# Moving one load in a hand-written order: step 6's rows right behind step 4's

## The chip, the cores and the metric

The kernel runs on one core of one Trainium2 chip. The metric is the device time of one execution in microseconds (us), lower is better. The core has five engines with queues of their own: TensorE (PE in the profile; its weight loads are PEld), VectorE (DVE), ScalarE (ACT), GpSimd (POOL) and SyncE (SP). Each runs its instructions strictly in the order in which the program was written; they meet only through semaphores. Transfers between the chip's main memory and its on-chip memory are issued by SyncE, GpSimd and once by ScalarE, and are carried by 16 DMA engines.

## The reference

A 3x3 convolution with zero padding, 64 channels in and 128 out, on 16 images of 64x64, then a 2x2 maximum pool:

```python
for b, co, ci, kh, kw:                       # conv is [16, 128, 64, 64]
    conv[b, co] += weight[co, ci, kh, kw] * x_pad[b, ci, kh:kh+h, kw:kw+w]
...
output[b, c, i, j] = np.max(conv[b, c, 2*i:2*i+2, 2*j:2*j+2])   # [16, 128, 32, 32]
```

## The kernel before

Two images share the 128 partitions (2 x 64 channels). The work is cut into 32 steps; a step is a pair of images and a quarter of the rows (16 rows of input, 8 rows of pooled output), and its two images are its halves 0 and 1. The even and the odd rows of a step's convolution differ only in which taps meet which rows, so the kernel multiplies sums and differences of input rows with sums and differences of taps instead of computing both rows in full. There are two kinds of steps, by the string `TYPES`:

- K steps (0, 2, 5, 7, 10, ...) read rows that were cast to bf16 on the way in (`kx`, loaded by `LK` through GpSimd's queue), and need one row sum, `KS` (line 356, VectorE).
- W steps (1, 3, 4, 6, 8, 9, 11, 12, ...) read f32 rows (`wx`, loaded through SyncE's queue at line 137) and make three bf16 operands of them: `E`, the difference of even and odd rows (line 407; on VectorE for steps 3, 8, 9 and 15, on GpSimd for the others), `D`, the difference of rows two apart (line 416, GpSimd), and `WS`, the sum of even and odd rows (VectorE, lines 374, 387 or 395). For steps 4, 6, 8, 14, 17, 22 and 23 ScalarE first copies the odd rows into a bank of PSUM (`XC`, line 370), and `WS` adds that copy (line 374).

Two successive W steps share one of six `wx` buffers: 1 and 3, 4 and 6, 8 and 9, 11 and 12, 14 and 15, 16 and 17; then the buffers are used again (19 and 20 in the first, 22 and 23 in that of 4 and 6). The load of the first of a pair has 18 rows (17 at the top of an image), that of the second 16 (15 at the bottom).

TensorE (line 252) runs the products `PA1`, `PA2`, `PB1`, `PB2`, `PR` of K steps and `P2`, `P0`, `P3`, `P1` of W steps; each is three matmuls of one half, and a product of half 0 is issued interleaved with the next product of half 1, so a pair of products is six matmuls. There are eight banks of PSUM. `EV` (lines 468 and 470, ScalarE) copies a bank out and frees it, `SE` (481, ScalarE) seeds another, `MX` (498, VectorE) takes the maximum of even and odd rows, `OD` (502, ScalarE) copies odd columns out, `CM` (508, VectorE) takes the maximum over columns and frees the bank, and `ST` (516, 519, SyncE) stores the result. A product that starts a bank waits for whoever freed it: P2.4.0 for EV.5.1, for instance, and P2.6.1 for CM.5.1. The numbers are the step and the half.

The order of all this is one text, `ORDER`, written out by hand: a token a step of work, and each engine gets its instructions in the order of the tokens. Loads are `L` and `LB`, both `wload` (line 129). `LB` adds one wait: the load is issued behind the VectorE operation that was last put on record (`on_vector`, line 87: `KS`, the halves `Ea` and `Eb` of step 1's `E`, the `E` of VectorE, and `WS` of line 395 among them) where the token stands. A `D` or `E` of GpSimd waits for the last recorded VectorE operation in the same way (`on_gpsimd`). The W loads before the change come in the order 1, 3, 11, 4, 8, 6, 9, 14, 12, 16, 22, 20 and so on; `LB.4` waits for `KS.0`, `LB.8` and `LB.6` both for `Eb`, and `LB.9` for `E.3`.

```python
def late_load(s):
    behind(wload(s), sbuf_op[0])
```

The products of the first two steps are written in halves (`F`, `G`). Of the steps around the moved load, ScalarE runs OD.3.1, XC.6, XC.4, EV.5.1 in this order; VectorE runs CM.1.1, CM.2.1, CM.3.1, WS.6, WS.4, KS.5, WS.9, KS.7, CM.3.0; GpSimd runs E.4, D.4, E.6, LK.1.0, D.8, D.6, D.9.

Of the kernel before, what the change touches and what calls it, by code (L numbers as in the profile page):

```python
# [11 lines left out]
def kernel(  # L12
# [556 lines left out]

    ORDER = """  # L570
        g2 D2 g0 TD2 D0 TD0 XOa TG0 VD2 F.0.0 GS TG2 g1 XOb VG0 GM F.1.0 uG1 XEb LB.3 VD0 F.0.1 F.1.1 GP VG2 XEa
        EV.0.1 L.11 X2 X1 LK.0.0 uGM F.2.0 PA1.2.0 KS.0 LB.4 Ea uGP F.3.0 TG1 KS.2 F.2.1 TMP Eb F.3.1 PA1.2.1
# [3 lines left out]
        SE.3.0 P0.3.0 EV.3.1 MX.1.1 P3.3.1 P1.1.1 OD.2.0 MX.2.1 E.11 P3.3.0 MX.3.1 ST.0 PR.2.1 P1.3.1 OD.1.0
        EV.3.0 PA1.5.0 PA1.5.1 E.4 OD.1.1 CM.2.0 CM.1.0 MX.3.0 CM.1.1 OD.2.1 PA2.5.1 PB1.5.0 P1.3.0 L.14 PB2.5.0
        D.4 OD.3.1 XC.6 PA2.5.0 E.6 CM.2.1 L.12 P2.4.1 P2.4.0 CM.3.1 XC.4 PA1.7.0 LK.1.0 EV.5.1 PB1.5.1 WS.6
        PB2.5.1 WS.4 L.16 SE.4.1 OD.3.0 PA2.7.0 P0.4.1 KS.5 P3.4.1 WS.9 KS.7 D.8 EV.5.0 SE.4.0 PA1.7.1 CM.3.0
        EV.4.1 EV.7.0 P0.4.0 PA2.7.1 MX.5.1 D.6 P3.4.0 MX.5.0 PR.5.0 MX.4.1 P2.6.0 PR.5.1 EV.4.0 PB1.7.0 MX.4.0  # L580
        XC.8 E.8 P1.4.1 EV.7.1 OD.5.1 P1.4.0 PB1.7.1 OD.4.1 WS.8 PB2.7.1 D.9 OD.5.0 PB2.7.0 SE.6.0 CM.5.1 CM.4.1
        P0.6.0 CM.5.0 OD.4.0 P2.6.1 SE.6.1 MX.7.1 P2.8.1 L.22 MX.7.0 EV.6.0 L.20 CM.4.0 SE.8.1 P3.6.0 PR.7.0
        PR.7.1 P0.6.1 OD.7.1 MX.6.0 EV.6.1 OD.7.0 P2.8.0 E.9 P3.6.1 SE.8.0 P0.8.1 CM.7.1 P1.6.0 P3.8.1 MX.6.1
        E.12 EV.8.1 CM.7.0 P2.9.0 ST.2 OD.6.0 CM.6.0 SE.9.0 P0.8.0 P1.6.1 ST.4 MX.8.1 P3.8.0 P2.9.1 EV.8.0 ST.5
        MX.8.0 L.19 P0.9.0 D.11 P2.11.0 OD.6.1 L.15 CM.6.1 PA1.13.1 P1.8.1 EV.9.0 ST.6 L.25 KS.13 P1.8.0 SE.9.1
        PA2.13.1 SE.11.0 P3.9.0 LK.1.1 KS.10 P0.11.0 D.12 E.14 P0.9.1 OD.8.0 WS.11 EV.13.1 P3.11.0 MX.9.0 P3.9.1
        PA1.10.1 D.14 P1.9.0 OD.8.1 EV.9.1 CM.8.0 CM.8.1 MX.9.1 EV.11.0 P2.12.1 XC.14 PA2.10.1 OD.9.0 MX.11.0
        P1.9.1 L.17 PA1.13.0 E.19 SE.12.1 CM.9.0 P2.11.1 PA2.13.0 P0.12.1 P1.11.0 EV.10.1 EV.13.0 P2.14.0
        PA1.10.0 OD.9.1 WS.14 PA2.10.0 SE.11.1 P3.12.1 P0.11.1 WS.12 EV.12.1 CM.9.1 OD.11.0 MX.12.1 P3.11.1
        P1.12.1 SE.14.0 CM.11.0 ST.1 EV.11.1 P2.12.0 E.15 SE.12.0 P0.14.0 PB1.10.1 P3.14.0 PB2.10.1 MX.11.1  # L590
        EV.14.0 E.16 MX.14.0 D.16 P0.12.0 XC.22 P1.11.1 P3.12.0 P1.14.0 EV.10.0 L.24 EV.12.0 P2.14.1 PB1.10.0
        D.15 WS.22 ST.3 OD.11.1 PB1.13.1 MX.10.1 PB2.10.0 PB2.13.1 MX.12.0 OD.12.1 CM.11.1 P1.12.0 OD.14.0 L.23
        CM.12.1 CM.14.0 SE.14.1 PR.10.1 PA1.21.0 E.17 P0.14.1 MX.13.1 MX.10.0 PA2.21.0 OD.12.0 PR.13.1 PR.10.0
        OD.10.1 CM.10.1 XC.17 EV.14.1 CM.12.0 OD.13.1 WS.17 P3.14.1 EV.21.0 OD.10.0 CM.13.1 P2.15.1 L.27 MX.14.1
        P2.15.0 P2.16.1 PA1.18.0 L.28 SE.15.0 CM.10.0 P1.14.1 PA2.18.0 SE.15.1 P0.15.1 E.20 SE.16.1 ST.12.0 ST.12.1
        P0.15.0 EV.18.0 WS.16 OD.14.1 P3.15.0 WS.15 P3.15.1 P0.16.1 KS.18 EV.15.0 LK.2.0 ST.10 PB1.13.0 P2.16.0
        CM.14.1 EV.15.1 MX.15.0 MX.15.1 EV.16.1 P3.16.1 SE.16.0 PB2.13.0 P2.17.1 MX.16.1 P1.15.1 P1.15.0 SE.17.1
        P0.16.0 OD.15.1 MX.13.0 P1.16.1 PR.13.0 EV.16.0 P3.16.0 D.17 WS.20 P0.17.1 P3.17.1 OD.16.1 P2.17.0
        CM.15.1 CM.16.1 MX.16.0 PA1.18.1 ST.11 OD.13.0 P2.19.0 EV.17.1 PA2.18.1 OD.15.0 CM.13.0 P1.16.0 SE.17.0
        EV.18.1 P0.17.0 P2.20.1 P3.17.0 OD.16.0 D.20 SE.20.1 MX.17.1 PB1.18.0 P1.17.1 D.19 CM.15.0 EV.17.0  # L600
        PA1.21.1 CM.16.0 WS.19 SE.19.0 P0.20.1 E.24 OD.17.1 MX.17.0 E.23 PA2.21.1 EV.20.1 PB2.18.0 MX.18.0
        P3.20.1 ST.7 P0.19.0 P1.17.0 PB1.18.1 EV.21.1 PR.18.0 XC.23 OD.17.0 CM.17.1 P2.19.1 MX.20.1 E.22 P3.19.0
        P2.20.0 EV.19.0 D.23 OD.18.0 WS.23 PB2.18.1 CM.17.0 CM.18.0 P2.23.0 SE.19.1 MX.19.0 MX.18.1 P1.20.1
        OD.20.1 ST.15 P0.19.1 P1.19.0 KS.21 L.31 P3.19.1 SE.20.0 P0.20.0 EV.19.1 D.22 P3.20.0 PR.18.1 OD.19.0
        ST.8.0 ST.8.1 SE.23.0 P0.23.0 CM.20.1 P2.22.1 MX.19.1 EV.20.0 P3.23.0 CM.19.0 OD.18.1 SE.22.1 MX.20.0 P1.19.1
        D.24 CM.18.1 P1.20.0 EV.23.0 PB1.21.1 OD.19.1 P0.22.1 PB2.21.1 OD.20.0 MX.23.0 CM.19.1 P2.22.0 P1.23.0
        CM.20.0 P2.23.1 ST.16.0 ST.16.1 ST.13 EV.22.1 MX.21.1 PB1.21.0 ST.19 SE.22.0 KS.26 ST.17 P0.22.0 L.30 PB2.21.0
        SE.23.1 WS.28 P3.22.1 PR.21.1 OD.23.0 CM.23.0 E.27 P0.23.1 P3.23.1 P2.24.0 EV.22.0 MX.22.1 EV.23.1
        MX.21.0 P3.22.0 OD.21.1 P1.22.1 SE.24.0 OD.22.1 P2.24.1 PR.21.0 MX.23.1 P0.24.0 E.25 OD.21.0 P3.24.0
        P1.23.1 CM.21.1 SE.24.1 CM.22.1 ST.20.0 ST.20.1 EV.24.0 D.25 D.27 MX.22.0 P2.25.1 OD.23.1 D.28 P0.24.1 CM.21.0  # L610
        SE.25.1 P3.24.1 WS.24 CM.23.1 E.28 P1.22.0 OD.22.0 CM.22.0 ST.23 PA1.26.0 PA2.26.0 P0.25.1 WS.25 P2.25.0
        P3.25.1 EV.24.1 EV.26.0 EV.25.1 PB1.26.0 MX.24.1 PA1.26.1 MX.25.1 PA2.26.1 SE.25.0 PB2.26.0 P2.27.1
        MX.26.0 P1.25.1 EV.26.1 P0.25.0 EV.25.0 P3.25.0 SE.27.1 MX.24.0 PR.26.0 P1.24.1 P0.27.1 OD.25.1 P3.27.1
        OD.24.1 OD.26.0 P1.24.0 OD.24.0 MX.25.0 CM.25.1 P2.27.0 CM.24.1 P1.25.0 CM.26.0 ST.22 P2.28.1 EV.27.1
        WS.27 PB1.26.1 E.30 PB2.26.1 CM.24.0 SE.27.0 OD.25.0 P2.28.0 SE.28.1 CM.25.0 SE.28.0 E.31 P0.27.0
        MX.27.1 P0.28.1 P1.27.1 P3.28.1 EV.27.0 MX.26.1 P3.27.0 ST.21 EV.28.1 MX.27.0 P0.28.0 D.30 PR.26.1
        P3.28.0 OD.27.1 P1.27.0 EV.28.0 ST.25 CM.27.1 P2.30.0 MX.28.1 PA1.29.0 P2.30.1 OD.26.1 CM.26.1 OD.27.0
        P1.28.1 SE.30.0 PA1.29.1 KS.29 OD.28.1 CM.27.0 PA2.29.0 P0.30.0 PA2.29.1 SE.30.1 MX.28.0 P0.30.1 EV.29.0
        ST.26 P1.28.0 P2.31.1 P3.30.0 EV.29.1 OD.28.0 CM.28.1 EV.30.0 P2.31.0 WS.31 CM.28.0 P3.30.1 D.31 WS.30
        EV.30.1 PB1.29.1 MX.30.0 PB2.29.1 ST.24 PB1.29.0 MX.30.1 PB2.29.0 MX.29.0 SE.31.0 ST.18 SE.31.1 MX.29.1  # L620
# [50 lines left out]
```

## Time and profile before

| | us |
|---|---|
| median of 3 runs (lowest, highest) | 104.76 (104.11, 105.74) |
| the profiled execution, its own time | 104.74 |
| its span, first to last instruction | 102.9 |
| TensorE busy | 96.5 (94%) |
| VectorE busy | 90.0 (87%) |
| ScalarE busy | 86.0 (84%) |
| GpSimd busy | 79.8 (77%) |
| mean traffic of the DMA engines | 236 GB/s, 24.25 MB |

The profile is one execution on the chip, with a start and a length for every instruction and the semaphores that released it. "A <- B: total, times, longest" says that A waited for B. A line of the timeline has the start, the length, the engine, the line of the code, the operation, output and inputs, the count of instructions merged into it, and in brackets how long the engine had stood idle before and what ended that. A busy TensorE isn't TensorE at its peak, since matmuls overlap in its pipeline. A list of DMA issues gives the median time from issue to landing, the landing being the last of the 16 engines' reports.

### The profile page before, as it was taken

Reading aid. Unit: us, or ns where it says so; the run is one execution under the profiler, and the core shown is the slowest. Engines: PE = TensorE matmul, PEld = TensorE weight load, DVE = VectorE, ACT = ScalarE, POOL = GpSimd, SP = SyncE. Lnnn points to the kernel's source line nnn. Section 1 sums busy time; section 2 is a strip of 40 time slices with the busy share of each in tenths; the row PEclk is TensorE's granted clock in tenths of the full one; section 3 lists DMA queues with packets and bytes.
Section 4 is the critical chain, followed back from the end, with each engine's and each line's share of the span. In section 5 each row is a group of like instructions: output and inputs, shape, how many; then the busy total and the mean of one; then the engine's idle time right before and its main releaser. Section 6 shows DMA issues by size and latency. Waiting matters only on the chain.

```text
span 102.9 us, 2528 instructions
## 1 busy us (share of the span) xinstructions
PE 96.5 (94%) x904; PEld 58.8 (57%) x904; DVE 90.0 (87%) x175; ACT 86.0 (84%) x192; POOL 79.8 (77%) x67
## 2 busy tenths in 40 slices
...
DMA packets 13789, 24.25 MB, mean 236 GB/s; under 512 B 1104, under 2 KB 9296, under 8 KB 13776
## 3 DMA queue, kind: packets, MB, share of 16 engines
...
q0 software_dynamic: 1104, 2.23, 13.4%
q8 instruction: 7, 0.11, 0.5%
...
HBM read 17.92 MB, written 8.39 MB: 256 GB/s over the span
## 4 chain that ended last, share of the span: by engine, by line
PE 78%; DMA 10%; DVE 3%; ACT 3%; issue 1%; DVEq 0%; SPq 0%; ACTq 0%
PE acc L252 73%; DMA wx<-in_x_dram 10%; PE acc L628 3%; PE acc L198 2%; DVE o L508 1%; ACT ev L468 1%; ACT kx L533 1%; DVE acc L498 1%; ACT acc L370 1%; DVE ks L356 0%; DVE we L407 0%; DVE we L428 0%; DVEq L666 0%; SPq L137 0%; DVEq L498 0%
## 5 line engine op out<-in xcount | busy, mean ns | idle before, releaser
L252 PEld LDWEIGHTS <-wt 64*128 64x128 bf16 x870 | 55.8, 94 | 35.2 <-issue 3.3
L252 PE MATMUL acc<-wd,wt 64*128 64x504 bf16 (+3 forms) x276 | 53.9, 367 | 0.0
L416 POOL TENSOR_TENSOR wd<-wx 128x1024 bf16<-128x1024 f32 x21 | 49.3, 2361 | 3.3 <-DVE ks L356 3.1
L252 PE MATMUL acc<-kx,wt 64*128 64x504 bf16 (+6 forms) x264 | 45.0, 351 | 0.0
L498 DVE TENSOR_TENSOR acc<-acc,ev 128x512 f32<-128x512 f32 x64 | 42.0, 689 | 1.6 <-PE acc L252 1.1
L252 PE MATMUL acc<-we,wt 64*128 64x512 bf16 (+3 forms) x138 | 31.8, 367 | 1.3 <-ACT ev L468 1.2
L252 PE MATMUL acc<-ws,wt 64*128 64x512 bf16 (+1 forms) x132 | 32.5, 377 | 0.0
L470 ACT ACTIVATE ev<-acc 128x512 f32<-128x512 f32 x44 | 26.2, 611 | 2.1 <-PE acc L252 1.7
L481 ACT COPY acc<-acc 128x512 f32<-128x512 f32 x42 | 24.5, 593 | 1.9 <-PE acc L252 0.9
L508 DVE TENSOR_TENSOR o<-acc,od 128x256 f32<-128x256 f32 x64 | 24.9, 414 | 1.1 <-ACT od L502 0.9
L502 ACT COPY od<-acc 128x256 f32<-128x256 f32 x64 | 23.2, 384 | 2.5 <-PE acc L252 2.0
L407 POOL TENSOR_TENSOR we<-wx 128x512 bf16<-128x512 f32 x17 | 21.4, 1273 | 4.4 <-PE acc L252 3.8
L252 PE MATMUL acc<-ks,wt 64*128 64x504 bf16 (+1 forms) x60 | 13.6, 377 | 0.0
L468 ACT COPY ev<-acc 128x512 f32<-128x512 f32 x20 | 11.8, 601 | 1.9 <-PE acc L252 1.7
L387 DVE TENSOR_REDUCE ws<-wx 128x512 bf16<-128x1024 f32 x9 | 11.1, 1229 | 0.0
L374 DVE TENSOR_TENSOR ws<-wx,acc 128x512 bf16<-128x512 f32 x7 | 4.7, 677 | 1.5 <-ACT acc L370 1.5
L370 ACT COPY acc<-wx 128x512 f32<-128x512 f32 x7 | 4.2, 602 | 1.6 <-DMA wx<-in_x_dram 1.6
L356 DVE TENSOR_TENSOR ks<-kx 128x512 bf16<-128x512 bf16 x10 | 4.4, 449 | 0.6 <-ACT kx L533 0.6
L395 DVE TENSOR_TENSOR ws<-wx 128x512 bf16<-128x512 f32 x6 | 4.5, 764 | 0.0
L628 PE MATMUL acc<-const-bfloat16-1.0 128*128 128x512 bf16 x8 | 3.6, 625 | 0.8 <-PEq L652 0.8
L443 POOL TENSOR_TENSOR wd<-wx 128x512 bf16<-128x512 f32 x2 | 2.5, 1262 | 1.8 <-DVE we L428 1.8
L227 ACT CAST wq<-wraw 128x192 bf16<-128x192 f32 x3 | 1.5, 535 | 1.7 <-DMA wraw<-in_weight_dram 1.7
...
## 6 DMA issues: line engine op xcount, KB each, us to landing
...
wx<-in_x_dram SPq DMA_DIRECT2D x8, 512.0 KB, 9.4
wx<-in_x_dram SPq DMA_DIRECT2D x7, 576.0 KB, 8.3
...
```

The costliest lines, as they stand in the source:

```text
L252: nc.tensor.matmul(acc[t][:, i0:i1, o0:o1], wt[lo : lo + CI, tap_of(m0, kw, h), :], rows(lo, i0, i1, c0, c1), start=start and kw == 1, sto ...
L370: nc.scalar.copy(out=acc[copied[s]], in_=t[:, f + 1 : f + 2 * R : 2, :])
L387: nc.vector.tensor_reduce(out=row["ws", s], in_=t[:, f : f + 2 * R, :].rearrange("p (r two) w -> p r w two", two=2), axis=mybir.AxisListTy ...
L407: inst = (nc.vector if vector else nc.gpsimd).tensor_tensor(out=row["we", s], in0=t[:, f : f + 2 * R : 2, :], in1=t[:, f + 1 : f + 2 * R : ...
L416: nc.gpsimd.tensor_tensor(out=row["wd", s], in0=t[:, f + 1 : f + 1 + 2 * R, :], in1=t[:, f - 1 : f - 1 + 2 * R, :], op=SUB)
L468: nc.scalar.copy(out=ev[s, h], in_=acc[t])
L470: nc.scalar.mul(ev[s, h], acc[t], -1.0)
L481: nc.scalar.copy(out=acc[t], in_=acc[ta[s, h]])
L498: nc.vector.tensor_tensor(out=t, in0=t, in1=ev[s, h], op=MAX)
L502: nc.scalar.copy(out=od[s, h], in_=acc[tb[s, h]][:, :, 1::2])
L508: nc.vector.tensor_tensor(out=ot[s][:, h], in0=acc[t][:, :, 0::2], in1=od[s, h], op=MAX)
L628: nc.tensor.matmul(acc[n].rearrange("p a b -> p (a b)"), ones[:, 0:128], ones, start=True, stop=True, skip_group_check=True)
```

## The change

One token moves. `LB.6`, the load of step 6's rows (16 rows of two images, 512 KB), stood behind `Db`, after `LB.8`; now it stands right behind `LB.4`, ahead of `Ea`, `Eb` and `LB.8`. The operation last recorded there is `KS.0`, so `LB.6` waits for `KS.0` where it waited for `Eb`. `LB.8` keeps its place among the other tokens and its wait for `Eb`. All other lines of the diff are the same tokens, wrapped anew.

```diff
-        EV.0.1 L.11 X2 X1 LK.0.0 uGM F.2.0 PA1.2.0 KS.0 LB.4 Ea uGP F.3.0 TG1 KS.2 F.2.1 TMP Eb F.3.1 PA1.2.1
-        VMP LB.8 MX.0.1 EV.0.0 G.0.0 PA2.2.1 Da VG1 G.0.1 MX.0.0 SEa.0 SEa.1 Db LB.6 PA2.2.0 WS.1 SEb.1 PR.0.1
...
+        EV.0.1 L.11 X2 X1 LK.0.0 uGM F.2.0 PA1.2.0 KS.0 LB.4 LB.6 Ea uGP F.3.0 TG1 KS.2 F.2.1 TMP Eb F.3.1
+        PA1.2.1 VMP LB.8 MX.0.1 EV.0.0 G.0.0 PA2.2.1 Da VG1 G.0.1 MX.0.0 SEa.0 SEa.1 Db PA2.2.0 WS.1 SEb.1
...
```

More of the change, by code (lines that the diff above doesn't have):

```diff
@@ L571 @@
         g2 D2 g0 TD2 D0 TD0 XOa TG0 VD2 F.0.0 GS TG2 g1 XOb VG0 GM F.1.0 uG1 XEb LB.3 VD0 F.0.1 F.1.1 GP VG2 XEa
-        EV.0.1 L.11 X2 X1 LK.0.0 uGM F.2.0 PA1.2.0 KS.0 LB.4 Ea uGP F.3.0 TG1 KS.2 F.2.1 TMP Eb F.3.1 PA1.2.1
-        VMP LB.8 MX.0.1 EV.0.0 G.0.0 PA2.2.1 Da VG1 G.0.1 MX.0.0 SEa.0 SEa.1 Db LB.6 PA2.2.0 WS.1 SEb.1 PR.0.1
-        SEb.0 LK.0.1 E.3 PR.0.0 P2.3.1 PB1.2.1 EV.2.1 G.1.0 G.1.1 PB2.2.1 G.2.0 OD.0.0 G.2.1 EV.2.0 WS.3 EV.1.0
-        EV.1.1 PB1.2.0 PB2.2.0 CM.0.0 OD.0.1 SE.3.1 MX.1.0 CM.0.1 LB.9 D.3 MX.2.0 P2.3.0 P1.1.0 PR.2.0 P0.3.1
@@ L576 @@
[L576 to L620, printed above, removed]
@@ L621 @@
-        P0.31.0 P0.31.1 P3.31.1 ST.9 EV.31.0 P1.30.1 EV.31.1 PR.29.1 P3.31.0 MX.31.0 P1.30.0 PR.29.0 ST.28 ST.14
-        MX.31.1 OD.30.0 P1.31.0 OD.30.1 OD.29.0 ST.27 OD.29.1 CM.30.0 CM.30.1 P1.31.1 CM.29.0 ST.30 OD.31.0
-        OD.31.1 CM.29.1 ST.29 CM.31.0 ST.31.0 CM.31.1 ST.31.1
+        EV.0.1 L.11 X2 X1 LK.0.0 uGM F.2.0 PA1.2.0 KS.0 LB.4 LB.6 Ea uGP F.3.0 TG1 KS.2 F.2.1 TMP Eb F.3.1
+        PA1.2.1 VMP LB.8 MX.0.1 EV.0.0 G.0.0 PA2.2.1 Da VG1 G.0.1 MX.0.0 SEa.0 SEa.1 Db PA2.2.0 WS.1 SEb.1
@@ new lines @@
+        PR.0.1 SEb.0 LK.0.1 E.3 PR.0.0 P2.3.1 PB1.2.1 EV.2.1 G.1.0 G.1.1 PB2.2.1 G.2.0 OD.0.0 G.2.1 EV.2.0 WS.3
+        EV.1.0 EV.1.1 PB1.2.0 PB2.2.0 CM.0.0 OD.0.1 SE.3.1 MX.1.0 CM.0.1 LB.9 D.3 MX.2.0 P2.3.0 P1.1.0 PR.2.0
+        P0.3.1 SE.3.0 P0.3.0 EV.3.1 MX.1.1 P3.3.1 P1.1.1 OD.2.0 MX.2.1 E.11 P3.3.0 MX.3.1 ST.0 PR.2.1 P1.3.1
+        OD.1.0 EV.3.0 PA1.5.0 PA1.5.1 E.4 OD.1.1 CM.2.0 CM.1.0 MX.3.0 CM.1.1 OD.2.1 PA2.5.1 PB1.5.0 P1.3.0 L.14
+        PB2.5.0 D.4 OD.3.1 XC.6 PA2.5.0 E.6 CM.2.1 L.12 P2.4.1 P2.4.0 CM.3.1 XC.4 PA1.7.0 LK.1.0 EV.5.1 PB1.5.1
@@ new lines @@
+        WS.6 PB2.5.1 WS.4 L.16 SE.4.1 OD.3.0 PA2.7.0 P0.4.1 KS.5 P3.4.1 WS.9 KS.7 D.8 EV.5.0 SE.4.0 PA1.7.1
+        CM.3.0 EV.4.1 EV.7.0 P0.4.0 PA2.7.1 MX.5.1 D.6 P3.4.0 MX.5.0 PR.5.0 MX.4.1 P2.6.0 PR.5.1 EV.4.0 PB1.7.0
+        MX.4.0 XC.8 E.8 P1.4.1 EV.7.1 OD.5.1 P1.4.0 PB1.7.1 OD.4.1 WS.8 PB2.7.1 D.9 OD.5.0 PB2.7.0 SE.6.0 CM.5.1
+        CM.4.1 P0.6.0 CM.5.0 OD.4.0 P2.6.1 SE.6.1 MX.7.1 P2.8.1 L.22 MX.7.0 EV.6.0 L.20 CM.4.0 SE.8.1 P3.6.0
+        PR.7.0 PR.7.1 P0.6.1 OD.7.1 MX.6.0 EV.6.1 OD.7.0 P2.8.0 E.9 P3.6.1 SE.8.0 P0.8.1 CM.7.1 P1.6.0 P3.8.1
@@ new lines @@
+        MX.6.1 E.12 EV.8.1 CM.7.0 P2.9.0 ST.2 OD.6.0 CM.6.0 SE.9.0 P0.8.0 P1.6.1 ST.4 MX.8.1 P3.8.0 P2.9.1
+        EV.8.0 ST.5 MX.8.0 L.19 P0.9.0 D.11 P2.11.0 OD.6.1 L.15 CM.6.1 PA1.13.1 P1.8.1 EV.9.0 ST.6 L.25 KS.13
+        P1.8.0 SE.9.1 PA2.13.1 SE.11.0 P3.9.0 LK.1.1 KS.10 P0.11.0 D.12 E.14 P0.9.1 OD.8.0 WS.11 EV.13.1 P3.11.0
+        MX.9.0 P3.9.1 PA1.10.1 D.14 P1.9.0 OD.8.1 EV.9.1 CM.8.0 CM.8.1 MX.9.1 EV.11.0 P2.12.1 XC.14 PA2.10.1
+        OD.9.0 MX.11.0 P1.9.1 L.17 PA1.13.0 E.19 SE.12.1 CM.9.0 P2.11.1 PA2.13.0 P0.12.1 P1.11.0 EV.10.1 EV.13.0
@@ new lines @@
+        P2.14.0 PA1.10.0 OD.9.1 WS.14 PA2.10.0 SE.11.1 P3.12.1 P0.11.1 WS.12 EV.12.1 CM.9.1 OD.11.0 MX.12.1
+        P3.11.1 P1.12.1 SE.14.0 CM.11.0 ST.1 EV.11.1 P2.12.0 E.15 SE.12.0 P0.14.0 PB1.10.1 P3.14.0 PB2.10.1
+        MX.11.1 EV.14.0 E.16 MX.14.0 D.16 P0.12.0 XC.22 P1.11.1 P3.12.0 P1.14.0 EV.10.0 L.24 EV.12.0 P2.14.1
+        PB1.10.0 D.15 WS.22 ST.3 OD.11.1 PB1.13.1 MX.10.1 PB2.10.0 PB2.13.1 MX.12.0 OD.12.1 CM.11.1 P1.12.0
+        OD.14.0 L.23 CM.12.1 CM.14.0 SE.14.1 PR.10.1 PA1.21.0 E.17 P0.14.1 MX.13.1 MX.10.0 PA2.21.0 OD.12.0
@@ new lines @@
+        PR.13.1 PR.10.0 OD.10.1 CM.10.1 XC.17 EV.14.1 CM.12.0 OD.13.1 WS.17 P3.14.1 EV.21.0 OD.10.0 CM.13.1
+        P2.15.1 L.27 MX.14.1 P2.15.0 P2.16.1 PA1.18.0 L.28 SE.15.0 CM.10.0 P1.14.1 PA2.18.0 SE.15.1 P0.15.1 E.20
+        SE.16.1 ST.12.0 ST.12.1 P0.15.0 EV.18.0 WS.16 OD.14.1 P3.15.0 WS.15 P3.15.1 P0.16.1 KS.18 EV.15.0 LK.2.0 ST.10
+        PB1.13.0 P2.16.0 CM.14.1 EV.15.1 MX.15.0 MX.15.1 EV.16.1 P3.16.1 SE.16.0 PB2.13.0 P2.17.1 MX.16.1
+        P1.15.1 P1.15.0 SE.17.1 P0.16.0 OD.15.1 MX.13.0 P1.16.1 PR.13.0 EV.16.0 P3.16.0 D.17 WS.20 P0.17.1
@@ new lines @@
+        P3.17.1 OD.16.1 P2.17.0 CM.15.1 CM.16.1 MX.16.0 PA1.18.1 ST.11 OD.13.0 P2.19.0 EV.17.1 PA2.18.1 OD.15.0
+        CM.13.0 P1.16.0 SE.17.0 EV.18.1 P0.17.0 P2.20.1 P3.17.0 OD.16.0 D.20 SE.20.1 MX.17.1 PB1.18.0 P1.17.1
+        D.19 CM.15.0 EV.17.0 PA1.21.1 CM.16.0 WS.19 SE.19.0 P0.20.1 E.24 OD.17.1 MX.17.0 E.23 PA2.21.1 EV.20.1
+        PB2.18.0 MX.18.0 P3.20.1 ST.7 P0.19.0 P1.17.0 PB1.18.1 EV.21.1 PR.18.0 XC.23 OD.17.0 CM.17.1 P2.19.1
+        MX.20.1 E.22 P3.19.0 P2.20.0 EV.19.0 D.23 OD.18.0 WS.23 PB2.18.1 CM.17.0 CM.18.0 P2.23.0 SE.19.1 MX.19.0
@@ new lines @@
+        MX.18.1 P1.20.1 OD.20.1 ST.15 P0.19.1 P1.19.0 KS.21 L.31 P3.19.1 SE.20.0 P0.20.0 EV.19.1 D.22 P3.20.0
+        PR.18.1 OD.19.0 ST.8.0 ST.8.1 SE.23.0 P0.23.0 CM.20.1 P2.22.1 MX.19.1 EV.20.0 P3.23.0 CM.19.0 OD.18.1 SE.22.1
+        MX.20.0 P1.19.1 D.24 CM.18.1 P1.20.0 EV.23.0 PB1.21.1 OD.19.1 P0.22.1 PB2.21.1 OD.20.0 MX.23.0 CM.19.1
+        P2.22.0 P1.23.0 CM.20.0 P2.23.1 ST.16.0 ST.16.1 ST.13 EV.22.1 MX.21.1 PB1.21.0 ST.19 SE.22.0 KS.26 ST.17 P0.22.0
+        L.30 PB2.21.0 SE.23.1 WS.28 P3.22.1 PR.21.1 OD.23.0 CM.23.0 E.27 P0.23.1 P3.23.1 P2.24.0 EV.22.0 MX.22.1
@@ new lines @@
+        EV.23.1 MX.21.0 P3.22.0 OD.21.1 P1.22.1 SE.24.0 OD.22.1 P2.24.1 PR.21.0 MX.23.1 P0.24.0 E.25 OD.21.0
+        P3.24.0 P1.23.1 CM.21.1 SE.24.1 CM.22.1 ST.20.0 ST.20.1 EV.24.0 D.25 D.27 MX.22.0 P2.25.1 OD.23.1 D.28 P0.24.1
+        CM.21.0 SE.25.1 P3.24.1 WS.24 CM.23.1 E.28 P1.22.0 OD.22.0 CM.22.0 ST.23 PA1.26.0 PA2.26.0 P0.25.1 WS.25
+        P2.25.0 P3.25.1 EV.24.1 EV.26.0 EV.25.1 PB1.26.0 MX.24.1 PA1.26.1 MX.25.1 PA2.26.1 SE.25.0 PB2.26.0
+        P2.27.1 MX.26.0 P1.25.1 EV.26.1 P0.25.0 EV.25.0 P3.25.0 SE.27.1 MX.24.0 PR.26.0 P1.24.1 P0.27.1 OD.25.1
@@ new lines @@
+        P3.27.1 OD.24.1 OD.26.0 P1.24.0 OD.24.0 MX.25.0 CM.25.1 P2.27.0 CM.24.1 P1.25.0 CM.26.0 ST.22 P2.28.1
+        EV.27.1 WS.27 PB1.26.1 E.30 PB2.26.1 CM.24.0 SE.27.0 OD.25.0 P2.28.0 SE.28.1 CM.25.0 SE.28.0 E.31
+        P0.27.0 MX.27.1 P0.28.1 P1.27.1 P3.28.1 EV.27.0 MX.26.1 P3.27.0 ST.21 EV.28.1 MX.27.0 P0.28.0 D.30
+        PR.26.1 P3.28.0 OD.27.1 P1.27.0 EV.28.0 ST.25 CM.27.1 P2.30.0 MX.28.1 PA1.29.0 P2.30.1 OD.26.1 CM.26.1
+        OD.27.0 P1.28.1 SE.30.0 PA1.29.1 KS.29 OD.28.1 CM.27.0 PA2.29.0 P0.30.0 PA2.29.1 SE.30.1 MX.28.0 P0.30.1
```

5 lines of the change are left out of this document (added).

## The prediction, made before the change was run

> **What bounds the kernel now.** I read the chain of waits first, because it names the one place where TensorE, busy for most of the span, is held up from outside. Columns: start in us, length, what.
>
> ```profile
> span 102.9 us, 2528 instructions
> ...
> 10.11 0.33 SPq L137
> ...
> 10.49 10.62 DMA wx<-in_x_dram
> ...
> 21.18 0.04 ACT acc L370
> ...
> 21.71 0.58 ACT acc L370
> 22.29 0.52 ACT ev L468
> ...
> 22.86 9.24 PE acc L252 x82
> ...
> 32.90 64.07 PE acc L252 x586
> ```
>
> From 22.86 on the chain is TensorE, but for 0.8 us at 32.1. Ahead of it stands one transfer, issued at 10.49 and waited for until 21.1, whose rows ScalarE copies at line 370. That line is the copy of odd rows (XC); the first XC in the order is step 6's, so the transfer is L.6, the one that is moved. The waits between 15 and 30 us (total, times, longest) show what hangs on it:
>
> ```profile
> ACT acc L370 <- DMA wx<-in_x_dram: 1.6, 1, 1.6
> DVE ws L374 <- ACT acc L370: 1.5, 1, 1.5
> ...
> POOL wd L416 <- DVE ks L356: 1.3, 1, 1.3
> PE acc L252 <- ACT ev L468: 1.2, 1, 1.2
> ```
>
> ScalarE waits 1.6 us for L.6, VectorE 1.5 us for ScalarE's copy (WS.6 adds it), and TensorE 1.2 us for EV.5.1, which stands behind XC.6 and XC.4 on ScalarE and frees the bank that P2.4.0 takes. Behind this place TensorE has nothing left to win: the table by stretches (length, then busy time and count of PE, PEld, DVE, ACT, POOL, then the granted clock, DMA share and GB/s) has it full for 64 us, at clock 1.00.
>
> ```profile
> 24.00:31.00 7.00, 7.00 (x69) 4.12 (x67) 6.80 (x15) 6.50 (x15) 6.55 (x3) 1.00 0.74 157
> 33.00:97.00 64.00, 64.00 (x596) 40.42 (x596) 61.80 (x116) 57.96 (x131) 55.69 (x32) 1.00 0.72 221
> ```
>
> So the whole gain on offer is that one hole, and what is won there moves the end if TensorE and what feeds it all move with it.
>
> **The change, step by step.** Nothing is added or dropped: one DMA issue moves on SP's queue. SyncE's timeline gives the issues of LB.4, LB.8, LB.6 and LB.9, and the list of issues of the same windows (KB, us to landing) their landings, in the same order:
>
> ```profile
> 7.61 0.33 SPq L137 DMA_DIRECT2D wx<-in_x_dram  x1
> 10.11 0.33 SPq L137 DMA_DIRECT2D wx<-in_x_dram  x1
> 10.49 0.53 SPq L137 DMA_DIRECT2D wx<-in_x_dram  x1
> 13.31 0.33 SPq L137 DMA_DIRECT2D wx<-in_x_dram  x1
> ```
> ```profile
> wx<-in_x_dram SPq DMA_DIRECT2D x1, 576.0 KB, 9.6
> wx<-in_x_dram SPq DMA_DIRECT2D x1, 576.0 KB, 9.1
> wx<-in_x_dram SPq DMA_DIRECT2D x1, 512.0 KB, 10.6
> wx<-in_x_dram SPq DMA_DIRECT2D x1, 512.0 KB, 9.0
> ```
>
> Adding up: L.4 lands at 17.2, L.8 at 19.2, L.6 at 21.1, L.9 at 22.3. Transfers land in the order of issue, some 2 us apart, however long ago they were issued: the backlog sets the landing, and the issue time matters only as a place in line.
>
> *The issue.* A late load waits for the newest VectorE step on record when it is written. LB.4's is KS.0, and LB.6 inherits that; LB.8 keeps Eb (the second half of step 1's even-row difference).
>
> ```profile
> 7.17 0.41 DVE L356 TENSOR_TENSOR ks<-kx 128x512 bf16<-128x512 bf16 x1
> 9.66 0.42 DVE L428 TENSOR_TENSOR we<-wx 128x256 bf16<-128x256 f32 x1
> ```
>
> KS.0 is over at 7.58, so LB.6 goes out right behind LB.4, at about 8.0 instead of 10.49. LB.8 is still issued at 10.11 when Eb ends. The stretch of SP's queue between them is empty in both orders, so nothing waits behind the moved issue. Cost on SP: 0.33 to 0.53 us (its rows above), in time that SP spends waiting for Eb; without that cover LB.8 would go out up to 0.5 us late, still far ahead of its place in line. LB.9 and everything later keeps its place and its sum of bytes ahead, so L.9 still lands at 22.3.
>
> *The landing.* L.6 takes L.8's slot. That slot ended at 19.2 with 576 KB; L.6 has 512 KB, and by 512/576 of the 2.0 us between L.4 and L.8 it lands at 19.0. I take 19.0 to 19.2. L.8 then ends where L.6 did, at 21.1; its first user is step 8's difference D.8 on GpSimd (below), which started at 24.45. Swapping costs nothing there, with about 2.4 us to spare even if D.8 comes a us earlier.
>
> *ScalarE and TensorE.* What is next late once L.6 is there at 19.2?
>
> ```profile
> 19.22 0.37 ACT L502 COPY od<-acc 128x256 f32<-128x256 f32 x1 [0.19 <-PE acc L252]
> 21.18 1.11 ACT L370 COPY acc<-wx 128x512 f32<-128x512 f32 x2 [1.59 <-DMA wx<-in_x_dram]
> ```
> ```profile
> 20.24 0.38 PE L252 MATMUL acc<-we,wt 64*128 64x512 bf16 x1
> 20.46 0.38 PE L252 MATMUL acc<-we,wt 64*128 64x504 bf16 x1
> ...
> 20.72 0.98 PE L252 MATMUL acc<-kx,wt 64*128 64x504 bf16 x7
> 22.86 0.37 PE L252 MATMUL acc<-we,wt 64*128 64x512 bf16 x1 [1.16 <-ACT ev L468]
> ```
>
> ScalarE is done with its row of 19.22 at 19.59, so XC.6 starts at 19.6, 1.58 us earlier. From XC.6's start to EV.5.1's end are 22.81 - 21.18 = 1.63 us, so EV.5.1 is done at 21.23. TensorE starts a pair of matmuls every 0.22 us, six to a pair of products (0.65 us): products begin at 20.24, 20.89, and would at 21.54. The bank is free before that, so the hole goes whole: 22.86 - 21.54 = 1.32 us (the profile's own 1.16 is counted from the modelled end of the last matmul). It does not matter whether L.6 lands at 19.0 or 19.6.
>
> *VectorE, which gives a part back.* VectorE was idle behind XC.6 too, and it meets another transfer sooner now.
>
> ```profile
> 19.26 1.08 DVE L508 TENSOR_TENSOR o<-acc,od 128x256 f32<-128x256 f32 x3
> 21.80 1.28 DVE L374 TENSOR_TENSOR ws<-wx,acc 128x512 bf16<-128x512 f32 x2 [1.47 <-ACT acc L370]
> ...
> 23.34 0.68 DVE L395 TENSOR_TENSOR ws<-wx 128x512 bf16<-128x512 f32 x1
> ...
> 24.28 0.41 DVE L508 TENSOR_TENSOR o<-acc,od 128x256 f32<-128x256 f32 x1
> ...
> 28.20 1.08 DVE L508 TENSOR_TENSOR o<-acc,od 128x256 f32<-128x256 f32 x3
> ```
>
> WS.6 can start at 20.34, when the three column maxima end: 1.46 us earlier. WS.9 (line 395) follows 1.54 us behind it, at 21.88; but its rows are L.9, there at 22.3, and with the 0.07 us from L.6's landing to XC.6's start in the trace it begins at about 22.4. VectorE's gain is 23.34 - 22.4 = 0.94 us, and the row of the stretch 24 to 31 us has it busy 6.80 of 7.00, so it can't catch up there. Does TensorE feel that? The first of the three column maxima from 28.20 ends at 28.61 (0.41 each) and frees the bank of P2.6.1:
>
> ```profile
> 28.67 0.37 PE L252 MATMUL acc<-we,wt 64*128 64x512 bf16 x1
> ...
> 29.26 0.38 PE L252 MATMUL acc<-wd,wt 64*128 64x512 bf16 x1
> ```
>
> The gap is 0.06 us, so there TensorE can be no more than that ahead of VectorE, and its gain shrinks from 1.32 to something between 0.94 and 1.00 us. I take 0.95.
>
> *GpSimd.* D.8 waits for KS.7 on VectorE, so it starts 0.94 us earlier, and D.6 behind it ends earlier by as much.
>
> ```profile
> 17.29 1.28 POOL L407 TENSOR_TENSOR we<-wx 128x512 bf16<-128x512 f32 x1 [0.31 <-DMA wx<-in_x_dram]
> ...
> 22.39 0.75 POOL L114 DMA_DIRECT2D kx<-in_x_dram  x1
> 24.45 7.00 POOL L416 TENSOR_TENSOR wd<-wx 128x1024 bf16<-128x1024 f32 x3 [1.32 <-DVE ks L356]
> ```
>
> D.8, D.6 and D.9 take 7.00/3 = 2.33 us each: D.6 ended at 29.1, TensorE used it at 29.26 (P0.6.0, the row above). With 0.94 us on GpSimd and 0.16 to spare this allows TensorE 1.10, so VectorE's 0.95 holds. L.22, which overwrites the buffer of steps 4 and 6, waits for D.6 and moves up with it.
>
> *Sum.* 104.74 us of the profiled execution (102.9 us of span and 1.84 around it) less 0.95 gives 103.8. The median of the three runs, 104.76, is the same but for 0.02, so the figure stands against the median too.
>
> One rule of the Trainium skill, weighed against these rows: the page "DMA: Bandwidth & Descriptors", section "Anatomy of one DMA — SWDGE (gpsimd) path", fits a transfer as 2.0 us plus its bytes over 436 GB/s; an estimate from it for 512 KB is 3.2 us. By that L.6, issued at 10.49, would be there before 14 us, no engine would wait for it, and the sum would be 104.74. The trace has 10.6 us for it, so here the rule holds for a transfer alone and not for one behind a backlog.
>
> **The rivals.**
>
> *No gain.* TensorE's stall moves and isn't shortened: what XC.6 saves is taken up behind it, by L.9 landing later than its row says or by ScalarE and VectorE, each some 93 to 97% busy from 24 to 31 us. For it speaks that the gaps of 0.06 us above leave TensorE no slack of its own; against it that VectorE is ahead by 0.94 even after L.9. With half of VectorE's gain or more lost (L.9 at 22.8 or later, 0.5 us behind its row) it gives 104.3 to 104.7.
>
> *All of it.* L.9 lands early enough for WS.9 at 21.88, 0.4 us before its row. Then TensorE keeps 1.32 us and perhaps 0.2 of the 0.8 us that the chain spends off TensorE at 32.1: 103.2 to 103.4. Nothing in the rows speeds L.9 up.
>
> *Slower: the line isn't kept.* If the DMA engines share out time between all transfers outstanding on SP's queue, L.6, out 2.5 us earlier, takes time from L.4, whose user E.4 on GpSimd has none to spare (0.31 us of waiting in the row of 17.29). L.6's 512 KB are 1.8 us of queue time; L.4 would land at 19.0 at the earliest, and at 21.1 if it ended together with the two behind it. From E.4 GpSimd runs E.4, D.4, E.6 and a kx load's issue before D.8: 1.28 + 2.33 + 1.28 + 0.75 = 5.6 us by the rows of 17.29, 22.39 and 24.45. E.4 at 17.29 would allow D.8 at 22.9; it turns to a loss when L.4 lands after 18.8. At 19.0 D.8 starts some 0.2 us late and the time is 104.9; at 21.1 it is 2.3 late and, less the 0.16 to spare, the time is 106.9. Against it: L.8 and L.6 were both outstanding from 10.5 to 19.2, and L.8 landed a full 1.9 us ahead. The same page of the Trainium skill, section "Queues, rings and completion order", has each engine take the descriptors of a ring in order, and those landings agree.
>
> *The edit does nothing*, because L.6 is held on SP by something else than KS.0. The issue row at 10.49 stands directly behind LB.8's, and SP is idle between 7.94 and 10.11, so I see nothing that could hold it; this goes with no gain.
>
> **How the numbers follow.** A measurement of this kernel tells about 2%, or 2.1 us, from no change. Forecast 103.8, chance 0.70, its own range 103.4 to 104.2, from TensorE's 1.32 at one end and 0.55 at the other. All of it: 0.08. No gain: 0.14. Slower: 0.08, half of it by more than 2%. The three runs before lie from 104.11 to 105.74, so a median can be some tenths off. The range 103.1 to 104.9 takes in the forecast, the full gain, no gain and the near end of the slower case, and leaves out about 0.15. Faster by over 2% needs 102.6, just about the whole hole and those 0.8 us together, so only a lucky draw gives it: 0.04. Slower by over 2% needs 106.9, the far end of the slower case: 0.04. The rest, 0.92, lies within 2%.
>
> **What would show it.** In the profile after: LB.6 issued near 8.0 and landed near 19.0, LB.8 landed near 21.1; no wait of line 370 for a DMA; no TensorE hole near 22; in its place a VectorE wait of some 0.5 us of line 395 for a DMA near 22; D.8 on GpSimd near 23.5; TensorE's long run ending about 0.95 us earlier. I'd be wrong if L.4 or L.9 landed later than before, if D.8 didn't move, or if a new TensorE hole opened behind 31 us.

## The result, and the profile after

| | before | changed |
|---|---|---|
| median of 17 runs (lowest, highest), us | 104.62 (103.91, 107.02) | 103.84 (103.05, 104.65) |
| profiled execution, its span, us | 104.74, 102.9 | 103.84, 102.1 |

The ratio is 0.9912, 95% interval [0.9886, 0.9939]: 0.9% faster, or 0.9 us. The forecast was 103.8. The ratio is estimated from the fast runs alone, those within 1.5% of the fastest of the same kernel, so it isn't the quotient of the two medians, 0.9925.

The chain of waits of the changed kernel (start, length, what), where before it went through the transfer of L.6 and ScalarE's copy:

```profile
11.89 19.38 PE acc L252 x192
...
31.30 0.33 DVE we L407
31.63 0.35 DVE o L508
...
32.02 64.08 PE acc L252 x586
```

From 11.89 on it is TensorE alone, but for the same short trip through VectorE, which now ends at 32.02 and not at 32.90. The last stretch is as long as before (64.08 against 64.07 us), so what was won by 32 us was kept to the end. The longest waits between 15 and 33 us:

```profile
POOL we L407 <- PE acc L252: 1.1, 1, 1.1
...
ACT acc L481 <- PE acc L252: 0.7, 2, 0.4
POOL wd L416 <- DVE ks L356: 0.7, 1, 0.7
```

Line 370 waits for no transfer any more, and TensorE for no EV. SyncE's issues of LB.6, LB.8 and LB.9 in the changed kernel, and their landings (KB, us from issue) from the list of issues:

```profile
8.24 0.86 SPq L137 DMA_DIRECT2D wx<-in_x_dram  x1
10.62 0.33 SPq L137 DMA_DIRECT2D wx<-in_x_dram  x1
13.83 0.33 SPq L137 DMA_DIRECT2D wx<-in_x_dram  x1
```
```profile
wx<-in_x_dram SPq DMA_DIRECT2D x1, 512.0 KB, 11.3
wx<-in_x_dram SPq DMA_DIRECT2D x1, 576.0 KB, 10.5
wx<-in_x_dram SPq DMA_DIRECT2D x1, 512.0 KB, 8.6
```

L.6 lands at 19.5, L.8 at 21.1, L.9 at 22.4. L.6 went out 2.2 us earlier and took longer from issue to landing than before (11.3 against 10.6), as a transfer does that waits in line. The engines around the place, from the timeline:

```profile
20.01 1.14 ACT L370 COPY acc<-wx 128x512 f32<-128x512 f32 x2
...
20.78 1.27 DVE L374 TENSOR_TENSOR ws<-wx,acc 128x512 bf16<-128x512 f32 x2
21.97 0.59 DVE L356 TENSOR_TENSOR ks<-kx 128x512 bf16<-128x512 bf16 x1
22.51 0.69 DVE L395 TENSOR_TENSOR ws<-wx 128x512 bf16<-128x512 f32 x1
...
21.00 1.28 POOL L407 TENSOR_TENSOR we<-wx 128x512 bf16<-128x512 f32 x1
...
23.63 7.00 POOL L416 TENSOR_TENSOR wd<-wx 128x1024 bf16<-128x1024 f32 x3 [0.67 <-DVE ks L356]
...
20.76 0.38 PE L252 MATMUL acc<-we,wt 64*128 64x512 bf16 x1
...
21.97 0.38 PE L252 MATMUL acc<-we,wt 64*128 64x512 bf16 x1
```

The hole is gone: P2.4.1 starts at 20.76 and P2.4.0 at 21.97, 1.2 us behind it, where it was 2.6 us (20.24 and 22.86). Two things were not foreseen. P2.4.1 itself is 0.52 us later than before, so this execution came to the place late. And VectorE's sum of step 9 (line 395), which should have waited for L.9, follows its predecessor without a gap, while that predecessor, KS.5 (line 356), takes 0.59 us, where it took 0.42 before. L.9 landed only 0.1 us ahead of that sum, so this profile alone can't say which of the two set its start. The experiments take up both.

### The profile page after: what moved, and what is told of

Its sections match the earlier page's. It is cut to its first block, busy times and chain, and to the rows that moved or that the text cites. A ratio compares the mean times of both kernels' runs of the same rounds, so it can differ in the third digit from the quotient of the medians.

```text
span 102.1 us, 2528 instructions
## 1 busy us (share of the span) xinstructions
PE 96.0 (94%) x904; PEld 60.4 (59%) x904; DVE 90.6 (89%) x175; ACT 86.1 (84%) x192; POOL 79.6 (78%) x67
## 4 chain that ended last, share of the span: by engine, by line
PE 82%; DMA 7%; DVE 5%; SPq 2%; issue 1%; DVEq 0%
PE acc L252 82%; DMA wx<-in_x_dram 7%; DVE o L508 1%; DVE acc L498 1%; DVE we L428 1%; SPq L151 0%; SPq L145 0%; DVE ks L356 0%; SPq L144 0%; SPq L140 0%; PE acc L491 0%; DVEq L666 0%; DVE we L407 0%; DVE wt L221 0%; DVEq L498 0%
## 5 line engine op out<-in xcount | busy, mean ns | idle before, releaser
L252 PEld LDWEIGHTS <-wt 64*128 64x128 bf16 x870 | 57.8, 94 | 32.7 <-issue 3.0
```

What stands on the lines that cost most here:

```text
L252: nc.tensor.matmul(acc[t][:, i0:i1, o0:o1], wt[lo : lo + CI, tap_of(m0, kw, h), :], rows(lo, i0, i1, c0, c1), start=start and kw == 1, sto ...
```

## The experiments

All ratios are to the kernel before, run on the same chip, with 95% intervals. What the diffs show is tokens of the order, with ... for what lies between; everything else is as in the kernel named, but for the last pair of runs, which add six matmuls.

### Is the late start a part of the change?

The changed kernel was run again, unaltered, in two further comparisons.

> The changed kernel once more, unaltered, for a second profile. In the first one the first rows came late: the load of the first half of step 1 landed at 9.4 us (8.3 before) and TensorE reached the place of the old stall 0.5 us later than before. My theory: that lag belongs to the execution and not to the change, since the first rows land before the moved load is issued. Then the ratio is again 0.989 to 0.994, and the lag can be there or not; where it isn't, VectorE's sum of step 9 (line 395) waits some 0.4 us for its rows. Rival: the earlier issue slows the loads ahead of it; then the first half of step 1 lands near 9.4 us again.

0.9918 [0.9888, 0.9947].

> The changed kernel again, beside the next two on one chip, because the earlier place_only (0.9964) fell into its rival's range while its profile showed no wait for step 6's rows. Both theories: ratio 0.989 to 0.994. Where line 356's sum of step 5 runs beside GpSimd's difference of step 6, it ends some 0.28 us behind it, as in the profiles so far, and takes 0.55 us or more instead of 0.42.

0.9956 [0.9924, 0.9988], just above the range. All three intervals overlap, and all three say faster, by 0.9 us twice and by 0.5 us in the third. The table by stretches, 4 to 10 us (length, then busy time and count of PE, PEld, DVE, ACT, POOL, clock, DMA share, GB/s), of the changed kernel's first profile, and of its third:

```profile
4.00:10.00 6.00, 5.31 (x76) 3.72 (x77) 3.68 (x10) 4.63 (x11) 2.85 (x6) 1.00 0.98 312
```
```profile
4.00:10.00 6.00, 6.00 (x80) 4.09 (x79) 4.15 (x12) 5.04 (x12) 2.87 (x6) 1.00 0.96 314
```

In the first TensorE stood idle for 0.69 us there, and its chain ahead of 11.89 goes through the load of the first half of step 1, which landed at 9.4 (8.3 before); in the third it lost nothing, with the same order of loads. In the second it was idle for 0.71 us, and P2.4.1 started at 20.55. The expectation's reason was wrong, for L.6 is issued before those rows land (8.24 against 9.4). What speaks for the execution is that the old order of loads comes late too: in copy_swap, below, the same rows landed 7.5 us after their issue, against 5.7 in the profile of before and 6.2 to 6.8 in the three of the changed kernel, and TensorE lost 0.79 us. The third profile is thus the one to set beside that of before, which had no such loss either:

```profile
20.24 1.29 DVE L374 TENSOR_TENSOR ws<-wx,acc 128x512 bf16<-128x512 f32 x2
21.45 0.61 DVE L356 TENSOR_TENSOR ks<-kx 128x512 bf16<-128x512 bf16 x1
22.11 0.69 DVE L395 TENSOR_TENSOR ws<-wx 128x512 bf16<-128x512 f32 x1
...
23.05 0.42 DVE L508 TENSOR_TENSOR o<-acc,od 128x256 f32<-128x256 f32 x1
...
26.97 1.08 DVE L508 TENSOR_TENSOR o<-acc,od 128x256 f32<-128x256 f32 x3
...
20.50 1.27 POOL L407 TENSOR_TENSOR we<-wx 128x512 bf16<-128x512 f32 x1
...
20.10 0.38 PE L252 MATMUL acc<-we,wt 64*128 64x512 bf16 x1
...
21.32 0.38 PE L252 MATMUL acc<-we,wt 64*128 64x512 bf16 x1
...
27.44 0.37 PE L252 MATMUL acc<-we,wt 64*128 64x512 bf16 x1
```

From P2.4.1 to P2.4.0 it is 1.22 us. VectorE starts WS.6 1.56 us earlier than before (21.80), but CM.3.0 only 1.23 earlier (24.28 to 23.05), so it gave 0.33 us back in between, all of it between the start of KS.5 (1.56 earlier) and that of WS.9 (1.23 earlier). TensorE's P2.4.0 is 1.54 us earlier, but P2.6.1, which follows the first of the three column maxima by 0.06 us as it did before, only 1.23 (28.67 to 27.44): what VectorE gives back, TensorE loses there. The span was 101.7 us, 1.2 shorter.

### The moment of issue, or the place in line?

```diff
-        ... KS.0 LB.4 LB.6 Ea ... VMP LB.8 MX.0.1 ...
+        ... KS.0 LB.4 Ea ... VMP LB.6 LB.8 MX.0.1 ...
```

> Step 6's load ahead of step 8's, but with the old wait for Eb, so issued near 10.1 us and not near 8. My theory (the place in line counts, the moment of issue doesn't): it lands at 19.0 to 19.6 us, the copy of line 370 waits for no transfer, ratio 0.989 to 0.994 like the changed kernel. Rival (the early issue counts): the load lands 1 us or more later than in the changed kernel and the ratio is 0.995 to 1.000.

0.9964 [0.9936, 0.9992], in the rival's range. Its profile says otherwise: the issue, its landing, and ScalarE's copy, with no wait in front:

```profile
10.38 0.33 SPq L137 DMA_DIRECT2D wx<-in_x_dram  x1
...
19.77 1.15 ACT L370 COPY acc<-wx 128x512 f32<-128x512 f32 x2
```
```profile
wx<-in_x_dram SPq DMA_DIRECT2D x1, 512.0 KB, 8.2
```

L.6, issued at 10.38 as late as in the kernel before, lands at 18.6 and holds nobody up. Both kernels were then timed once more, side by side.

> Theory (place in line alone): no wait of line 370 for a transfer, ratio within 0.003 of the changed kernel beside it. Rival (the early issue is worth something of its own): 0.004 or more above it, and the profile shows step 6's rows or those behind them landing later than in the changed kernel.

0.9971 [0.9939, 1.0003], 0.0015 above the changed kernel in the same comparison, and again without a wait of line 370. Issued at 10.4 and 10.7, L.6 landed at 18.6 and 19.4 here; issued at 8.1 to 8.5 in the changed kernel, it landed at 18.3 to 19.5. The landing follows the place in line; that is shown. Whether the early issue is worth another 0.2 to 0.5% is not: both ratios lie that way, and the intervals overlap both times.

### Do step 9's rows cap the gain?

```diff
-        ... VMP LB.8 MX.0.1 ...  MX.1.0 CM.0.1 LB.9 D.3 ...
+        ... VMP LB.9 LB.8 MX.0.1 ...  MX.1.0 CM.0.1 D.3 ...
```

> The changed kernel with step 9's load ahead of step 8's too (order 4, 6, 9, 8). Step 9's rows land near 21.0 us instead of 22.3, step 8's near 22.4. My theory (step 9's rows cap the gain near 0.9 us): the sum of step 9 can start near 21.9, the gain grows to 1.2 to 1.4 us, ratio 0.986 to 0.988. Rival (something else caps it, the late first rows or VectorE's own work): ratio 0.990 to 0.993 as for the changed kernel.

0.9942 [0.9916, 0.9968], 0.0024 above the changed kernel in the same comparison, and far from the 0.986 to 0.988 of my theory. Issued at 10.27, the rows land 9.8 us later, at 20.1; the sum of step 9 starts at 22.13, in the timeline:

```profile
22.13 0.68 DVE L395 TENSOR_TENSOR ws<-wx 128x512 bf16<-128x512 f32 x1
```

> Theory as it stands after the first nine_first (step 9's rows do not cap the gain): ratio within 0.003 of the changed kernel beside it, and the sum of step 9 starts well behind its rows. Rival (they cap it in prompt executions): 0.003 or more below the changed kernel.

0.9939 [0.9902, 0.9975], 0.0017 below the changed kernel beside it. Its profile settles what the others left open, since in the third one L.9 had landed at 22.0, again just 0.1 us ahead of the sum:

```profile
22.07 0.60 DVE L356 TENSOR_TENSOR ks<-kx 128x512 bf16<-128x512 bf16 x1
22.73 0.69 DVE L395 TENSOR_TENSOR ws<-wx 128x512 bf16<-128x512 f32 x1
```

Here the rows were there at 21.2, 1.5 us ahead of the sum, and still it starts 0.66 us behind KS.5's start, as in the third profile (21.45 and 22.11), where before it was 0.33 (23.01 and 23.34). No time is won that could be measured. The rows of step 9 are not what caps the gain.

### Where VectorE gives time back: KS.5 beside E.6

In every profile with KS.5 beside GpSimd's E.6, KS.5 ends just behind E.6: in the changed kernel KS.5 at 22.56 and E.6 at 22.28, in its third profile at 22.06 and 21.77. Before, E.6 was over at 22.45 and KS.5 ran from 23.01, in 0.42 us. To test it, E.6 is moved behind KS.5:

```diff
-        ... PA2.5.0 E.6 CM.2.1 ...  P0.4.1 KS.5 P3.4.1 WS.9 KS.7 D.8 ...
+        ... PA2.5.0 CM.2.1 ...  P0.4.1 KS.5 E.6 P3.4.1 WS.9 KS.7 D.8 ...
```

> The changed kernel with GpSimd's difference of step 6 (E.6) moved behind VectorE's sum of step 5 (KS.5), which it then waits for; GpSimd issues the kx load first. My theory (a VectorE operation on rows in SBUF and a GpSimd one hold each other up): KS.5 takes 0.42 us again instead of 0.55 to 0.61, and the sum of step 9 or KS.7 behind it, now beside E.6, takes longer than its 0.68 or 0.42; so nothing is won, ratio 0.990 to 0.998. Rival (KS.5 is long for another reason, as late rows of kx): KS.5 still takes 0.55 us or more, the others keep their length.

1.001 [0.9981, 1.0039]; from its timeline:

```profile
21.36 0.41 DVE L356 TENSOR_TENSOR ks<-kx 128x512 bf16<-128x512 bf16 x1
21.70 0.68 DVE L395 TENSOR_TENSOR ws<-wx 128x512 bf16<-128x512 f32 x1
22.30 1.49 DVE L356 TENSOR_TENSOR ks<-kx 128x512 bf16<-128x512 bf16 x1
...
21.87 1.64 POOL L407 TENSOR_TENSOR we<-wx 128x512 bf16<-128x512 f32 x1 [0.80 <-DVE ks L356]
...
24.18 0.37 PE L252 MATMUL acc<-kx,wt 64*128 64x512 bf16 x1 [0.39 <-DVE o L508]
```

KS.5 is back at 0.41 us. Now E.6 overlaps WS.9 and takes 1.64 instead of 1.27, and KS.7, started beside E.6, takes 1.49 and ends at 23.79, again 0.28 behind E.6's end at 23.51. TensorE waits 0.39 us for VectorE, and the whole gain is lost, more than I had expected. That the two hold each other up is shown: the delay goes where the overlap goes. How much would be won with no overlap at all is not, for this edit moves the overlap and makes it longer, and no run takes it out of the changed kernel and leaves the rest as it was.

### How the time hangs on the landing of L.6

```diff
-        ... Db LB.6 PA2.2.0 ...  CM.0.1 LB.9 D.3 ...
+        ... Db PA2.2.0 ...  CM.0.1 LB.9 LB.6 D.3 ...
```

> The other way: step 6's load behind step 9's (order 4, 8, 9, 6). It lands near 22.4 us, 1.3 later than before. My theory (at this place the landing sets the time, one for one): TensorE's hole near 22 grows by 1.2 to 1.3 us, time 105.7 to 106.1, ratio 1.010 to 1.014. Rival (other work fills in, or another wait was about as late): less than half of that, ratio under 1.006.

1.0116 [1.007, 1.0163], from 6 runs; the ratio is as my theory had it. Its waits from 15 to 33 us:

```profile
ACT acc L370 <- DMA wx<-in_x_dram: 1.8, 1, 1.8
...
PE acc L252 <- ACT ev L468: 1.4, 1, 1.4
```

In this execution all loads landed early (L.9 at 20.1), and L.6, last in line, at 21.3, 0.2 us later than in the profile of before; the hole is 0.2 us wider too (1.4 against 1.2). That agrees with one for one, but 0.2 us isn't the 1.2 that I expected of the profile. A fairer partner is late_before, below, which has the old order of loads and whose L.4 and L.8 landed as early as here (16.3 and 17.7; here 16.3 and 17.6): its L.6 was there at 20.2, so L.6 is 1.1 us later here, and the ratio gives 1.2 us.

### Too far ahead

```diff
-        ... KS.0 LB.4 LB.6 Ea ...
+        ... KS.0 LB.6 LB.4 Ea ...
```

> The changed kernel with step 6's load ahead of step 4's as well (order 6, 4, 8, 9). Step 4's rows land near 18.5 to 19.0 us, 1.7 later. My theory (GpSimd's difference of step 4 has no time to spare): E.4 starts near 19, D.8 near 24.6 us, and the whole gain goes, ratio 0.998 to 1.004. Rival (GpSimd has slack there): ratio 0.989 to 0.994 as for the changed kernel.

1.0045 [1.0004, 1.0086], just above the range: the gain is gone, and a little more. The profiled execution, 106.21 us, lies above this kernel's median of 104.82, so its times are not set against those of the other kernels:

```profile
19.98 1.28 POOL L407 TENSOR_TENSOR we<-wx 128x512 bf16<-128x512 f32 x1 [2.32 <-DMA wx<-in_x_dram]
21.21 2.36 POOL L416 TENSOR_TENSOR wd<-wx 128x1024 bf16<-128x1024 f32 x1
...
22.15 1.70 DVE L356 TENSOR_TENSOR ks<-kx 128x512 bf16<-128x512 bf16 x1
```

E.4 waits 2.3 us for step 4's rows, which land at 19.9, later than the 18.5 to 19.0 that I expected, and have no time to spare, as the prediction had it. What it didn't have: D.4 and E.6 then run where VectorE does KS.5, which takes 1.70 us and ends 0.28 us behind D.4.

### ScalarE's queue, or the late rows themselves?

The order of loads of before, but with step 6's copy behind EV.5.1:

```diff
-        ... OD.3.1 XC.6 PA2.5.0 ... CM.3.1 XC.4 PA1.7.0 LK.1.0 EV.5.1 PB1.5.1 WS.6 PB2.5.1 WS.4 ...
+        ... OD.3.1 XC.4 PA2.5.0 ... CM.3.1 PA1.7.0 LK.1.0 EV.5.1 XC.6 PB1.5.1 WS.4 PB2.5.1 WS.6 ...
```

> The kernel before with its old order of loads, but ScalarE copies step 4's rows in the place of step 6's, and step 6's only behind EV.5.1; VectorE adds step 4 first too. The copy of step 6 still waits for the transfer to about 21 us, but EV.5.1 no longer stands behind it. My theory (VectorE is held up by the late rows as well, since its sum of step 6 needs that copy): TensorE's hole near 22 shrinks, and about 0.6 us are won, ratio 0.993 to 0.996. Rival (ScalarE's queue alone made the hole): all of the 0.9 to 1.3 us is won, ratio 0.988 to 0.991.

0.995 [0.9914, 0.9986], where my theory had it, though the interval takes in part of the rival's range. From its waits, and ScalarE's EV.5.1 and XC.6 in its timeline:

```profile
DVE ws L374 <- ACT acc L370: 0.7, 1, 0.7
```
```profile
21.60 0.59 ACT L468 COPY ev<-acc 128x512 f32<-128x512 f32 x1 [0.39 <-PE acc L252]
22.08 0.60 ACT L370 COPY acc<-wx 128x512 f32<-128x512 f32 x1
```

TensorE's wait for EV.5.1 is off the list, and VectorE waits 0.7 us for the copy of step 6's rows. But this execution, the longest of the twelve (104.63 us), says little of the cause. Its first rows came late, and P2.4.1 starts at 21.36, 1.1 us later than before. L.6 landed at 20.8, so by the 1.63 us from XC.6 to the end of EV.5.1 even the old order would have had the bank free at 22.5, and P2.4.0 started at 22.58. And the copy that VectorE waits for starts 1.3 us behind the landing, because it now stands behind EV.5.1: that wait isn't for late rows. What the ratio shows is that part of the hole's worth can be had by taking the waiting copy out of EV.5.1's way, without touching a load. That the hole came through ScalarE's queue rests on the chain of before; how much of it the late rows cost VectorE by themselves stays open.

### What the old hole was good for

Six matmuls of zeros are added onto step 3's banks in both orders; the sums stay the same.

> The kernel before with six matmuls of zeros added to step 3's banks, 0.65 us of TensorE's time near 15 us (the result stays the same). It stands for first rows that come late by so much. My theory (the old hole takes up any lateness ahead of it): the hole shrinks from 1.2 to about 0.5 us and the time is the same within 0.2 us, ratio 0.999 to 1.003. Rival (lateness is paid in full): plus 0.65 us, ratio 1.006.

1.0049 [1.0018, 1.008].

> The changed kernel with the same six matmuls of zeros. My theory (no hole is left to take up lateness, so the changed kernel pays in full what the kernel before did not): 0.5 to 0.65 us more than the changed kernel, ratio to the kernel before 0.996 to 1.000. Rival (step 9's rows or VectorE hold TensorE up there, so some lateness is still hidden): ratio 0.990 to 0.994, like the changed kernel alone.

1.0027 [0.9995, 1.006]. Both lie above what I expected: VectorE's maxima of step 3 came to stand behind the added matmuls (line 319 here), from the waits of the second kernel,

```profile
DVE acc L506 <- PE acc L319: 1.1, 1, 1.1
```

and P2.4.1 starts at 21.30 and 21.16, some 1.06 later than before and in the third profile, so the lateness is more than 0.65 us. Part of it can be first rows again: TensorE lost 0.77 and 0.25 us between 4 and 10 us. The kernel before then loses 0.5 us and the changed one about 1.0 (0.9929, the mean of its three ratios, to 1.0027), and both end up alike. In the first kernel's profile the hole is gone (P2.4.0 at 22.56, 1.26 behind P2.4.1), but there L.6 had landed at 20.2. All this agrees with a hole that took up part of the lateness. It isn't shown, since the rival's 1.006 lies in the first interval, and 0.5 and 1.0 differ by no more than the widths of the intervals.

## Why the prediction was right, point by point

- **What bounds it.** Right: the hole made by L.6 through XC.6 and EV.5.1. The time follows L.6's landing (six_last). That it does so through ScalarE's queue is in the chain of before; the ratio of copy_swap agrees.
- **Issue and landing.** Issued at 8.24 (forecast 8.0), landed at 19.5 (19.0 to 19.2), with L.8 at 21.1 and L.9 at 22.4 (21.1 and 22.3). In the other two profiles L.6 landed at 18.3 and 19.5. Each transfer took the slot of its place in line, and place_only shows that the issue time hardly counts. "Some 2 us apart" was loose: by the prediction's own rows L.9 came 1.2 us behind L.6.
- **ScalarE and TensorE, 1.32 us.** Right: 2.62 us between P2.4.1 and P2.4.0 became 1.21 to 1.29 in the three profiles, so 1.3 to 1.4 us went.
- **VectorE gives 0.38 us back: the coupling right, the cause wrong, the size near by luck.** The step read "its rows are L.9, there at 22.3". Those rows are not what was waited for; with them there 1.5 us ahead of the sum nothing measurable changed. VectorE gave back 0.19, 0.12 and 0.33 us in the three profiles, at KS.5, which now runs beside E.6. I had priced KS.5 at its old length without asking what would run beside it at its new place. That TensorE can be no further ahead than VectorE at P2.6.1 held in all three.
- **GpSimd.** D.8 moved by 0.82 us in the first profile (24.45 to 23.63) and by 1.22 in the third; 0.94 was forecast. That GpSimd has no time to spare behind L.4 was borne out by six_ahead_of_four; the size of its price was not tested.
- **The sum, 0.95 us.** The runs give 0.92 (0.9912 of 104.62), and 0.9 and 0.5 in the two repeats. So close a meeting is in part luck, since one of the two terms had the wrong cause and neither is a constant. The spans of the three profiles came out 0.8, 1.0 and 1.2 us shorter, the more the earlier P2.4.1 came. The old hole varies as well: in the three profiles with L.6 at its old place it landed at 21.1, 20.8 and 20.2.
- **The rivals.** Slower because the line isn't kept: it was kept in every profile, but late rows of step 4, its price, did cost the gain in six_ahead_of_four. No gain (104.3 to 104.7 of 104.74, a ratio of 0.9958 or more): excluded by the first two intervals, not by the third. All of it: near the 1.2 of the prompt execution, though no such median was measured.
